# Decode states loaded two steps ahead in a hybrid mLSTM and GLA layer, and side work handed out by a budget that carries its overdraft

## The chip, the cores and the metric

The kernel runs on one core of a Trainium2 chip. The metric is the device time of one execution in microseconds (us); the median of three runs of the kernel before is 846.66 us.

## The reference

One inference step of one layer for 256 prompt tokens and 8 decode tokens (one for each of 8 sequences), all in float32. `p = x @ w_in` feeds two recurrent branches; cut to what matters:

```python
# mLSTM branch: 4 heads, 256x256 matrix memory C for each head
qk = silu(conv(qk_pre)); q, k = split(qk); k = k * 256 ** -0.5
C_new = dec * C + einsum('bhs,bhsd,bhse->bhde', wk, k, v)
num   = decay * einsum('bhtd,bhde->bhte', q, C) + einsum('bhts,bhse->bhte', s, v)
h     = num / maximum(abs(den), exp(-m_t))
# GLA branch: 4 heads, 128x256 state S for each head, decay per key channel
S_new = exp(last) * S + einsum('bhsd,bhse->bhde', k * exp(last - bc), v)
o     = einsum('bhtd,bhde->bhte', q * exp(bc), S) + einsum('bhts,bhse->bhte', a, v)
# each branch: headwise norm, gate, projection; merge, output projection, layer norm
ya = (norm(h) * sigmoid(a_o) * silu(a_z)) @ w_pa
yb = (norm(o) * silu(b_z)) @ w_pb
y  = (sigmoid(g_a) * ya + sigmoid(g_b) * yb) @ w_out
out = layernorm(ALPHA * x + y)
```

For the 8 decode tokens the states C (8 x 4 x 256 x 256, 8 MB) and S (8 x 4 x 128 x 256, 4 MB) are read, updated with one token's key and value, multiplied with its query, and written back.

## The kernel before, in words

**Main work.** All tokens (264 columns: 256 prompt, 8 decode) stand as columns. The projections are 129 units, each one 128-row tile of outputs over 2048 inputs (the one called `small` is narrower): 16 `qk`, 1 `small`, 8 `av`, 4 `bq`, 4 `bk`, 8 `bv`, 16 `ao`/`az` in turns, 8 `bz`, 32 `ga`/`gb` in turns, 16 `pab`, 16 `out`; they are counted from 0 here. A unit's weights come as two pieces of 128x1024 float32. A piece goes through four engines: SP loads it (`load_raw`, line 181, tile `raw`, 4 buffers), ScalarE rounds it to the matmul's format (`hi`, line 203), VectorE takes the difference (`lo`, line 204), and TensorE multiplies hi by x_hi, hi by x_lo and lo by x_hi (lines 223, 224, 227): 48 matmuls a unit. Weights are cast three pieces (`LA`) ahead of the unit that uses them.

**Side work.** After each unit `pump(BUDGET)` runs the generators that are open, one step each, as long as the budget lasts; a step ends at a `yield`, which names its cost. Generators that are not in `BACK` go first, then up to `BACK_STEPS` (2) steps of the first one in `BACK`, which are the two decode generators. What a step overdraws is forgotten at the next unit:

```python
for g in [g for g in side if g.__name__ not in BACK]:
    if budget > 0:
        with tc.high_priority(offset=SIDE_PRIO):
            budget -= step(g)
```

The generators that matter here: `e_v`'s inner `g` transposes a value tile (`vT`, a ScalarE copy at line 394) on TensorE (line 401); `g_a_prompt` is the mLSTM of the prompt; `g_a_decode` the mLSTM decode (16 chunks of C, tile `cch`, scaled on ScalarE at line 546, updated and multiplied with the query on VectorE at lines 562 and 564); `g_gla_prompt` the GLA of the prompt, whose levels halve the tile: at each level TensorE multiplies at line 698 what VectorE scaled at line 705 in the step before; `g_gla_decode` the GLA decode (8 chunks of S, tile `sch`, four VectorE operations of 128x512 for each half chunk, lines 802 to 805); `g_a_norm` and `g_b_norm` the headwise norms (their statistics go through TensorE at lines 627, 639 and 824).

**What sets the order.** TensorE executes in the order of the program text (`MANUAL`): a side matmul stands behind the unit in whose pump it was issued. On the other engines and the DMA queues a scheduler orders instructions by priority before the kernel runs (`PRIO` 600 for casts, `SIDE_PRIO` 300 for side work outside `BACK`); on the chip each engine then goes through its list in order and waits where the next one isn't ready. Loads are issued by SP, stores of states (`sC`, `sS`, `pC`) by POOL.

**Memory.** Large tiles share the pool `b4` with `SLOTS` slots of 4 KB a partition (`t4`); tiles of 2 KB the tag `t2` with 5 buffers. A load into a slot waits until the slot's last user is done. Key and query rows of the decode tokens are written to DRAM and read back into all 128 partitions (`spread_rows`, line 283).

Of the kernel before, what the change touches and what calls it, by code (L numbers as in the profile page):

```python
# [13 lines left out]
F32 = mybir.dt.float32  # L14
# [3 lines left out]
ALU = mybir.AluOpType  # L18
# [16 lines left out]
BUDGET = 2.8  # L35
# [48 lines left out]
def body(ctx, tc, xT, wbig, wsmall, par, cmask, lmask, rowc, gate, wgu, cT, sT, nst, cst, lnr,  # L84
# [51 lines left out]
    wgu_sb = tmp.tile([16, 512], F32, tag="t2", name="wgu_sb", bufs=5)  # L136
    cst_sb = tmp.tile([128, KT, 3, NB], F32, tag="t2", name="cst_sb", bufs=5)
# [148 lines left out]
    def g_gates(ps):  # L286
# [66 lines left out]
        dm = one.tile([16, H, NB], F32, tag="dm", name="dm")  # L353
        V.tensor_tensor(out=dm, in0=r[:, L:T].unsqueeze(1).to_broadcast([16, H, NB]),
                        in1=rc_sb[0:16, 104:104 + H].unsqueeze(2).to_broadcast([16, H, NB]), op=ALU.mult)
        dr = one.tile([16, 2, NB], F32, tag="dr", name="dr")
        V.tensor_copy(out=dr[:, 0], in_=r[:, L:T])
        V.tensor_scalar(out=dr[:, 1], in0=wk[:, L:T], scalar1=K_SCALE, scalar2=None, op0=ALU.mult)
        yield 0.4
# [3 lines left out]
        PE.matmul(pb[:, 0:H * NB], lhsT=ones[0:16, :], rhs=dm.rearrange("p h b -> p (h b)"), start=True, stop=True)  # L363
# [21 lines left out]
    def e_v(ps, j, key, dkey):  # L385
# [23 lines left out]
    def g_a_prompt():  # L409
# [34 lines left out]
        def s3(h):  # L444
# [5 lines left out]
            kw = tmp.tile([128, 2, 256], F32, tag="t2", name="kw", bufs=5)  # L450
# [17 lines left out]
        for h in range(H + 1):  # L468
# [6 lines left out]
            yield 2.0  # L475
# [3 lines left out]
            yield 2.0  # L479
# [3 lines left out]
    def g_a_decode():  # L483
        qT, kT, dw, decb = st["qT"], st["kT"], st["dw"], st["decb"]
        num, dmx, avd = st["num"], st["dmx"], st["avd"]
# [5 lines left out]
        yield 0.5  # L491
        qr = tmp.tile([64, 128], F32, tag="t1", name="qr", bufs=T1_BUFS)
        kr = tmp.tile([64, 128], F32, tag="t1", name="kr", bufs=T1_BUFS)
        nr = tmp.tile([64, 128], F32, tag="t1", name="nr", bufs=T1_BUFS)
        pt = side_ps()
        for x in range(2):
            PE.transpose(out=pt[0:64, x * 128:x * 128 + 128], in_=qkd[:, x].rearrange("p h b t -> p (h b t)"), identity=ident)
        nc.sync.dma_start(out=nr, in_=nst)
        A.copy(out=qr, in_=pt[0:64, 0:128])
        V.tensor_scalar(out=kr, in0=pt[0:64, 128:256], scalar1=dw[:, 1:2], scalar2=None, op0=ALU.mult)  # L500
        kq_d = dram.tile([2, 64, 128], F32, name="kq_d")
        for x, src in enumerate((kr, qr)):
            nc.sync.dma_start(out=kq_d[x], in_=src)
        yield 0.5
# [7 lines left out]
        chunks = {}  # L512

        def load(i):
            if i < 16:
                c = t4([128, 4, 256], "cch")
                nc.sync.dma_start(out=c, in_=cT[i])
                chunks[i] = c

        load(0)  # L520
        yield 0.6
# [6 lines left out]
        yield 0.4  # L528
        scr2 = tmp.tile([128, 256], F32, tag="t1", name="scr", bufs=T1_BUFS)
        steps = [(h, b0, e) for h in range(H) for b0 in (0, 4) for e in range(2)]  # L530
        rows = {}

        def spread(i):

            if i < 16:
                h, b0, _ = steps[i]
                rows[h, b0] = t4([128, 4, 256], "kb"), t4([128, 4, 256], "qb")
                for x in range(2):
                    spread_rows(rows[h, b0][x], kq_d[x, 16 * h + 2 * b0:16 * h + 2 * b0 + 8, :])
# [8 lines left out]
        spread(0)  # L548
        scale(0)
        yield 1.6  # L550
        for i, (h, b0, e) in enumerate(steps):
            if e == 0:
                spread(i + 2)
            if i:
                G.dma_start(out=sC[i - 1], in_=chunks.pop(i - 1))
            if i + 1 < 16:
                scale(i + 1)
            kb, qb = rows[h, b0]
            c = chunks[i]
            nd = num.t(2 * h + e)  # L560
            for b in range(4):
                V.scalar_tensor_tensor(out=c[:, b, :], in0=kb[:, b, :], scalar=avd[:, 2 * h + e, b0 + b:b0 + b + 1],  # L562
                                       in1=c[:, b, :], op0=ALU.mult, op1=ALU.add)
                V.scalar_tensor_tensor(out=scr2, in0=c[:, b, :], scalar=1.0, in1=qb[:, b, :], op0=ALU.mult,  # L564
                                       op1=ALU.mult, accum_out=nd[:, L + b0 + b:L + b0 + b + 1])
                if b % 2:
                    yield 2.1
        G.dma_start(out=sC[15], in_=chunks.pop(15))
# [46 lines left out]
    def g_a_norm():  # L615
# [8 lines left out]
        for h in range(H):  # L624
# [4 lines left out]
            sq = tmp.tile([128, 2, T], F32, tag="t2", name="nsq", bufs=5)  # L629
# [23 lines left out]
    def g_gla_rows():  # L653
        gq, gk, la = st["gq"], st["gk"], st["la"]
        gd = one.tile([128, 3, H, NB], F32, tag="gd", name="gd")
        A.activation(out=gd[:, 0], in_=la[:, :, L:T], func=AF.Exp, scale=TAU_INV)
        V.tensor_copy(out=gd[:, 1], in_=gk[:, :, L:T])
        V.tensor_copy(out=gd[:, 2], in_=gq[:, :, L:T])
        yield 0.4
        pt = side_ps()  # L660
        PE.transpose(out=pt[0:96, 0:128], in_=gd.rearrange("p x h b -> p (x h b)"), identity=ident)
# [7 lines left out]
    def g_gla_prompt():  # L669
# [19 lines left out]
        for l in range(7):  # L689
# [16 lines left out]
            B2 = tmp.tile([128, H, n2], F32, tag="t2", name="gB", bufs=5)  # L706
            V.tensor_tensor(out=B2, in0=Bv[:, :, :, 0], in1=Bv[:, :, :, 1], op=ALU.add)
            E = tmp.tile([128, H, n2], F32, tag="t2", name="gE2", bufs=5)
            A.activation(out=E, in_=B2, func=AF.Exp, scale=TAU_INV)
            B, nb = B2, n2  # L710
            if hs == 32:
                for s0, n0 in ((0, 0), (64, 32)):
                    A.copy(out=am[s0:s0 + 32, :, s0 + 32:s0 + 64], in_=pl[s0:s0 + 32, :, n0:n0 + 32])
                yield 2.0
                continue
            if hs == 64:
                A.copy(out=am[0:64, :, 64:128], in_=pl[0:64])
                yield 2.0
# [8 lines left out]
            yield 3.0  # L727
# [3 lines left out]
        a01 = tmp.tile([128, 4, 128], F32, tag="t2", name="a01", bufs=5)  # L731
# [12 lines left out]
        for hh in range(2):  # L744
# [6 lines left out]
            pc = tmp.tile([128, 512], F32, tag="t2", name="pc", bufs=5)  # L751
# [14 lines left out]
    def g_gla_decode():  # L766
# [9 lines left out]
        load(0)  # L776
        yield 0.1
        spread = {}

        def rows_of(h):  # L780
            if h < H:
                spread[h] = [t4([128, NB, 128], "g" + x) for x in "akq"]
                for i, x in enumerate(spread[h]):
                    spread_rows(x, rows[32 * i + 8 * h:32 * i + 8 * h + 8, :])

        rows_of(0)
        yield 0.1
        for h in range(H):
            rows_of(h + 1)
            ab, kb, qb = spread.pop(h)  # L790
            for bh in range(2):
                load(2 * h + bh + 1)
                c = chunks.pop(2 * h + bh)
                b0 = 4 * bh
                for p in (0, 2):
                    q, cc, sh = slice(b0 + p, b0 + p + 2), c[:, p:p + 2], [128, 2, 2, 128]
                    kv, pr = (tmp.tile(sh, F32, tag="t2", name=x, bufs=5) for x in ("gkv", "gpr"))
                    for i in range(2):
# [500 lines left out]
```

## Time and profile before

| what | value |
|---|---|
| runs, us | 845.08, 846.66, 847.56 (median 846.66) |
| profiled execution, us | 846.17 |
| its span, first to last instruction, us | 844.3 |
| TensorE busy in the span | 819.3 us (97%) |
| VectorE busy | 592.8 us (70%) |
| ScalarE busy | 450.1 us (53%) |
| DMA traffic | 186.30 MB, mean 221 GB/s |

The profile takes one execution apart; what follows is read against its 844.3 us of span, and 1.87 us lie around the span. "Wait" means time in which an engine stood still in front of an instruction, and the row names what ended it. The clock column is the TensorE clock that was granted, 1.00 being 2.4 GHz.

### The profile page before, as it was taken

Reading aid. Unit: us, or ns where it says so; the run is one execution under the profiler, and the core shown is the slowest. Engines: PE = TensorE matmul, PEld = TensorE weight load, DVE = VectorE, ACT = ScalarE, POOL = GpSimd, SP = SyncE. Lnnn points to the kernel's source line nnn. Section 1 sums busy time; section 2 is a strip of 40 time slices with the busy share of each in tenths; the row PEclk is TensorE's granted clock in tenths of the full one; section 3 lists DMA queues with packets and bytes.
Section 4 is the critical chain, followed back from the end, with each engine's and each line's share of the span. In section 5 each row is a group of like instructions: output and inputs, shape, how many; then the busy total and the mean of one; then the engine's idle time right before and its main releaser. Section 6 shows DMA issues by size and latency. Waiting matters only on the chain.

```text
span 844.3 us, 16681 instructions
## 1 busy us (share of the span) xinstructions
PE 819.3 (97%) x6749; PEld 809.2 (96%) x6749; DVE 592.8 (70%) x967; ACT 450.1 (53%) x700; POOL 45.8 (5%) x75
## 2 busy tenths in 40 slices
PE   6999999999999899999999999899999999999996
PEld 6999999999999899999999999799999999999995
DVE  6977668655748888767489979984445676666962
ACT  5755457545544653555376758564444444444633
POOL 0000000000100000000000000400000000000410
PEclk9999999999999999999999999999999999999998
DMA  9765555867679985678776987665555555576513
GB/s 318 252 193 183 159 187 172 233 201 266 227 262 291 339 305 184 227 244 305 250 273 180 354 319 258 200 203 186 177 182 189 179 177 179 188 250 205 180 47 103
DMA packets 55237, 186.30 MB, mean 221 GB/s; under 512 B 8292, under 2 KB 9256, under 8 KB 55160
## 3 DMA queue, kind: packets, MB, share of 16 engines
q1 hardware_dynamic: 51032, 170.82, 62.3%
q0 software_dynamic: 4128, 14.42, 4.3%
q8 instruction: 53, 0.87, 0.4%
q14 instruction: 24, 0.20, 0.1%
HBM read 168.50 MB, written 16.71 MB: 219 GB/s over the span
## 4 chain that ended last, share of the span: by engine, by line
PE 79%; DMA 8%; DVE 7%; issue 3%; ACT 1%; SPq 0%; POOL 0%; ACTq 0%; POOLq 0%; DVEq 0%
PE mm L223 25%; PE mm L224 24%; PE mm L227 24%; DMA cch<-cT 4%; DVE lo L204 3%; DMA raw<-wbig 2%; DMA sch<-sT 2%; DMA pC<-pc 1%; DVE scr L564 1%; DVE gpr L804 1%; PE sd L698 1%; ACT hi L203 1%; DVE cch L562 1%; DVE sch L803 1%; ACT cch L546 0%
## 5 line engine op out<-in xcount | busy, mean ns | idle before, releaser
L223 PE MATMUL mm<-xh,hi 128*128 128x264 f32 x1552 | 446.8, 288 | 7.3 <-ACT hi L203 7.3
L224 PE MATMUL mm<-xl,hi 128*128 128x264 f32 x1552 | 440.9, 285 | 0.0
L227 PE MATMUL mm<-xh,lo 128*128 128x264 f32 x1536 | 436.9, 284 | 0.0
L203 ACT CAST hi<-raw 128x1024 fp32r<-128x1024 f32 (+1 forms) x260 | 267.8, 1034 | 288.3 <-PE mm L224 243.3
L204 DVE TENSOR_TENSOR lo<-raw,hi 128x1024 fp32r<-128x1024 f32 (+1 forms) x260 | 315.1, 1214 | 139.2 <-ACT hi L203 137.2
L223 PEld LDWEIGHTS mm<-xh,hi 128*128 128x128 f32 x1552 | 293.8, 189 | 8.9 <-ACT hi L203 7.3
L224 PEld LDWEIGHTS mm<-xl,hi 128*128 128x128 f32 x1552 | 293.9, 189 | 0.3
L227 PEld LDWEIGHTS mm<-xh,lo 128*128 128x128 f32 x1536 | 289.7, 189 | 0.2 <-DVE lo L204 0.2
L223 PE MATMUL mm<-mh,hi 128*128 128x264 f32 x256 | 72.9, 285 | 0.0
L227 PE MATMUL mm<-mh,lo 128*128 128x264 f32 x256 | 72.6, 284 | 0.0
L224 PE MATMUL mm<-ml,hi 128*128 128x264 f32 x256 | 72.4, 283 | 0.0
L224 PEld LDWEIGHTS mm<-ml,hi 128*128 128x128 f32 x256 | 48.1, 188 | 0.0
L223 PEld LDWEIGHTS mm<-mh,hi 128*128 128x128 f32 x256 | 48.1, 188 | 0.0
L227 PEld LDWEIGHTS mm<-mh,lo 128*128 128x128 f32 x256 | 48.1, 188 | 0.0
L546 ACT ACTIVATE cch<-cch,decb 128x256 f32<-128x256 f32 x64 | 27.8, 500 | 35.1 <-DMA cch<-cT 35.1
L562 DVE SCALAR_TENSOR_TENSOR cch<-kb,avd,cch 128x256 f32<-128x256 f32 x64 | 29.5, 480 | 20.4 <-ACT cch L546 17.8
L227 PE MATMUL mm<-ybh,lo 128*128 128x264 f32 x128 | 36.4, 284 | 0.0
L227 PE MATMUL mm<-yah,lo 128*128 128x264 f32 x128 | 36.3, 284 | 0.0
L224 PE MATMUL mm<-ybl,hi 128*128 128x264 f32 x128 | 36.3, 284 | 0.0
L223 PE MATMUL mm<-ybh,hi 128*128 128x264 f32 x128 | 36.3, 284 | 0.0
L223 PE MATMUL mm<-yah,hi 128*128 128x264 f32 x128 | 36.3, 284 | 0.0
L224 PE MATMUL mm<-yal,hi 128*128 128x264 f32 x128 | 36.2, 283 | 0.0
(310 smaller groups left out, 807.2 us busy)
## 6 DMA issues: line engine op xcount, KB each, us to landing
raw<-wbig SPq DMA_DIRECT2D x252, 512.0 KB, 4.7
cch<-cT SPq DMA_DIRECT2D x16, 512.0 KB, 8.8
sC<-cch POOLq DMA_DIRECT2D x16, 512.0 KB, 5.7
kb<-kq_d SPq DMA_DIRECT2D x8, 512.0 KB, 7.4
qb<-kq_d SPq DMA_DIRECT2D x8, 512.0 KB, 8.0
sch<-sT SPq DMA_DIRECT2D x8, 512.0 KB, 7.4
sS<-sch POOLq DMA_DIRECT2D x8, 512.0 KB, 6.0
xr<-xT SPq DMA_DIRECT2D x4, 528.0 KB, 6.9
```

Source lines behind the costliest of these rows:

```text
L203: A.copy(out=h, in_=r)
L204: V.tensor_tensor(out=lo, in0=r, in1=f(h), op=ALU.subtract)
L223: PE.matmul(out, lhsT=wh, rhs=rh, start=(k == k0), stop=False)
L224: PE.matmul(out, lhsT=wh, rhs=rl, start=False, stop=small and k == k1 - 1)
L227: PE.matmul(out, lhsT=los[n, k], rhs=rh, start=False, stop=(k == k1 - 1))
L546: A.activation(out=c[:, b, :], in_=c[:, b, :], func=AF.Copy, scale=decb[:, h, b0 + b:b0 + b + 1])
L562: V.scalar_tensor_tensor(out=c[:, b, :], in0=kb[:, b, :], scalar=avd[:, 2 * h + e, b0 + b:b0 + b + 1], in1=c[:, b, :], op0=ALU.mult, op1=A ...
L564: V.scalar_tensor_tensor(out=scr2, in0=c[:, b, :], scalar=1.0, in1=qb[:, b, :], op0=ALU.mult, op1=ALU.mult, accum_out=nd[:, L + b0 + b:L + ...
L698: PE.matmul(pl[s0:s0 + m, 4 * hf + h, n0:n0 + w].rearrange("p (n s) -> p n s", s=hs), lhsT=K[:, h, hf * 128 + s0:hf * 128 + s0 + m], rhs=r ...
L803: V.tensor_tensor(out=cc, in0=cc, in1=kv, op=ALU.add)
L804: V.tensor_tensor(out=pr, in0=cc, in1=qb[:, q].unsqueeze(2).to_broadcast(sh), op=ALU.mult)
```

## The change

It sets `SLOTS` 20 to 19, `T2_BUFS` 5 to 7, `BUDGET` 2.8 to 3.4. `pump` carries a negative rest over to the next unit (`credit`), and a step of a `BACK` generator with a negative cost ends the pump at once. In the mLSTM decode a chunk now holds 2 sequences with both halves of a head's values (before: 4 sequences with one half); its key and query rows come in one tile `kq` for each chunk (before: `kb` and `qb` for every second chunk). The chunk's load is issued two steps ahead of its use instead of one, that of its rows one chunk ahead; the scale of a chunk is 2 ScalarE instructions of 128x512 instead of 4 of 128x256. The key is no longer scaled by `K_SCALE * wk`; that factor goes into `avd`. In the GLA decode a chunk's rows come as `gak` (decay and key, 512 KB) and `gqr` (query, 256 KB, from `t2`) instead of `ga`, `gk`, `gq` (512 KB each) for two chunks, and chunks are loaded two steps ahead instead of one. `e_v`'s `g` yields twice with cost 0 before the transposes instead of once, `g_a_prompt` yields 1.5 instead of 2.0, the levels of `g_gla_prompt` 2.5 and 1.7 instead of 3.0 and 2.0, `g_g` 0.3 instead of 1.9.

```diff
-BUDGET = 2.8
+BUDGET = 3.4
-SLOTS = 20
+SLOTS = 19
+T2_BUFS = 7
...
     def e_v(ps, j, key, dkey):
...
         def g():
+            yield 0.0
             yield 0.0
             pt = side3(2, 128)
...
     def g_a_decode():
...
+        kqo = tmp.tile([128, 16, 2, 4], F32, tag="t1", name="kqo", bufs=T1_BUFS)
+        for x in range(2):
+            V.tensor_copy(out=kqo[:, :, x, :], in_=qkd[:, 1 - x].rearrange("p h (c b) t -> p (h c) (b t)", b=2))
+        V.tensor_tensor(out=avd.rearrange("p (h e) b -> p h e b", e=2), in0=avd.rearrange("p (h e) b -> p h e b", e=2),
+                        in1=wkb.unsqueeze(2).to_broadcast([128, H, 2, NB]), op=ALU.mult)
+        yield -0.5
...
+        PE.transpose(out=pt[:, 256:384], in_=kqo.rearrange("p a x c -> p (a x c)"), identity=ident)
...
+        load(0)
+        load(1)
+        yield -0.6
...
+        spread(0)
+        yield -1.0
         pb = side_ps()[:, 0:H * NB]
         PE.matmul(pb, lhsT=ones[0:64, :], rhs=dx, start=True, stop=True)
...
-            load(i + 1)
-            c = chunks[i]
-            for b in range(4):
-                A.activation(out=c[:, b, :], in_=c[:, b, :], func=AF.Copy, scale=decb[:, h, b0 + b:b0 + b + 1])
...
+                for b in range(2):
+                    A.activation(out=chunks[i][:, b], in_=chunks[i][:, b], func=AF.Copy, scale=decb[:, h, b0 + b:b0 + b + 1])
...
+        for i in range(16):
+            h, b0 = i // 4, i % 4 * 2
             if i:
-                G.dma_start(out=sC[i - 1], in_=chunks.pop(i - 1))
...
+                G.dma_start(out=sC[i - 1], in_=chunks.pop(i - 1).rearrange("p b e k -> p (b e) k"))
+            load(i + 2)
+            spread(i + 1)
+            scale(i + 1)
...
+                yield 2.1
...
     def g_gla_decode():
...
+                spread[i] = t4([128, 2, 4, 128], "gak"), tmp.tile([128, 4, 128], F32, tag="t2", name="gqr", bufs=T2_BUFS)
...
+        for i in range(8):
+            h, b0 = i // 2, i % 2 * 4
+            rows_of(i + 1)
+            load(i + 2)
...
+    credit = [0.0]
+
     def pump(budget):
+        credit[0] = budget = min(credit[0], 0.0) + budget
...
                 if budget > 0:
-                    budget -= step(g)
+                    c = step(g)
+                    budget -= abs(c)
+                    if c < 0:
+                        credit[0] = budget
+                        return
+        credit[0] = budget
```

How the change moves instructions shows at three places. The first is TensorE after unit 28 (`bq3`), where the small matmul that sums the decode normaliser (`dx`) stands at the end of the prompt's side work. Before:

```order
L435 MATMUL sd<-E,avt 128x256
L436 MATMUL sd<-E,avt 128x128
L437 MATMUL sd<-E,ones 128x256
L438 MATMUL sd<-E,ones 128x128
L461 MATMUL sd<-avt,kw 128x257 x4
L523 MATMUL sd<-dx,ones 128x32
```

Now, at the same place and, behind 48 + 7 + 48 further matmuls and the next head's first steps, after unit 30:

```order
L439 MATMUL sd<-E,avt 128x128
L440 MATMUL sd<-E,ones 128x256
L441 MATMUL sd<-E,ones 128x128
L464 MATMUL sd<-avt,kw 128x257 x4
L505 MATMUL sd<-par_sb,kqo 128x128
L507 MATMUL sd<-par_sb,qkd 64x128 x2
...
L441 MATMUL sd<-E,ones 128x128
L464 MATMUL sd<-avt,kw 128x257 x4
L540 MATMUL sd<-dx,ones 128x32
```

The matmul of `dx` has moved two units back, and the transposes of the query and key rows stand where it was.

The second is ScalarE over the `bv` units, where the copies `vT` stand between casts (`hi`) and the scales of the mLSTM chunks (`cch`). Before:

```order
L203 CAST hi<-raw 128x1024
L546 ACTIVATE cch<-cch,decb 128x256 x4
L203 CAST hi<-raw 128x1024
L394 COPY vT<-mm 128x256
L546 ACTIVATE cch<-cch,decb 128x256
L203 CAST hi<-raw 128x1024
L546 ACTIVATE cch<-cch,decb 128x256 x3
L203 CAST hi<-raw 128x1024
L394 COPY vT<-mm 128x256
L546 ACTIVATE cch<-cch,decb 128x256 x4
```

Now:

```order
L204 CAST hi<-raw 128x1024 x2
L396 COPY vT<-mm 128x256
L204 CAST hi<-raw 128x1024
L551 ACTIVATE cch<-cch,decb 128x512 x2
L204 CAST hi<-raw 128x1024
L396 COPY vT<-mm 128x256
L551 ACTIVATE cch<-cch,decb 128x512 x2
```

Between the casts each copy had up to eight scales, of two chunks, ahead of it; now one chunk's two scales stand between two copies, but they still stand ahead of the copy.

The third is SP's queue over the same units, with the loads of weights (`raw`), of chunks (`cch`) and of row tiles. Before:

```order
L181 DMA raw<-wbig 128x1024 x5
L517 DMA cch<-cT 128x1024
L283 DMA kb<-kq_d 128x1024
L283 DMA qb<-kq_d 128x1024
L517 DMA cch<-cT 128x1024
L181 DMA raw<-wbig 128x1024 x2
L517 DMA cch<-cT 128x1024
```

Now:

```order
L182 DMA raw<-wbig 128x1024 x6
L519 DMA cch<-cT 128x1024
L284 DMA kq<-kq_d 128x1024
L519 DMA cch<-cT 128x1024
L284 DMA kq<-kq_d 128x1024
L182 DMA raw<-wbig 128x1024 x4
L519 DMA cch<-cT 128x1024
L284 DMA kq<-kq_d 128x1024
```

Four loads of decode data still stand together between loads of weights; each is still 512 KB.

## Rows read from the trace of the kernel before

**Rows 1.** The page: busy time of the engines, share of the span, instructions.
```profile
PE 819.3 (97%) x6749; PEld 809.2 (96%) x6749; DVE 592.8 (70%) x967; ACT 450.1 (53%) x700; POOL 45.8 (5%) x75
```
**Rows 2.** All waits of TensorE: engine, line, what ended the wait, us in total, times, longest.
```profile
PE mm L223 <- ACT hi L203: 7.3, 1, 7.3
PE sd L824 <- DVE ns L819: 3.6, 2, 2.5
PE sd L401 <- ACT vT L394: 3.4, 2, 2.5
PE sd L698 <- DVE gq L705: 2.6, 1, 2.6
PE sd L523 <- ACT pnn L464: 0.8, 1, 0.8
```
**Rows 3.** Stretches of 20 us: busy us and instructions of PE, PEld, DVE, ACT, POOL, then granted clock, DMA share, GB/s.
```profile
260.00:280.00 20.00, 17.41 (x143) 16.99 (x141) 13.36 (x34) 9.20 (x16) 1.07 (x2) 1.00 0.92 325
280.00:300.00 20.00, 19.16 (x147) 19.16 (x148) 19.53 (x49) 11.96 (x20) 1.59 (x3) 0.91 0.95 334
440.00:460.00 20.00, 20.00 (x168) 20.00 (x167) 20.00 (x23) 12.49 (x18) 0.53 (x1) 1.00 0.65 207
460.00:480.00 20.00, 20.00 (x168) 20.00 (x167) 20.00 (x28) 13.45 (x25) 0.53 (x1) 1.00 0.87 303
520.00:540.00 20.00, 16.45 (x127) 15.66 (x126) 19.76 (x23) 14.66 (x26) 8.35 (x8) 1.00 0.74 233
560.00:580.00 20.00, 20.00 (x168) 20.00 (x167) 10.53 (x10) 10.36 (x14) 0.00 (x0) 1.00 0.64 206
```
**Rows 4.** TensorE in order of time from 277.9 to 285.7: start, us, line, what; in brackets the idle time before it and what ended it.
```profile
278.04 0.28 PE L227 MATMUL mm<-xh,lo 128*128 128x264 f32 x1
280.84 0.44 PE L401 MATMUL sd<-par_sb,vT 128*128 128x128 f32 x2 [2.52 <-ACT vT L394]
281.24 0.28 PE L224 MATMUL mm<-xl,hi 128*128 128x264 f32 x1
281.36 0.29 PE L227 MATMUL mm<-xh,lo 128*128 128x264 f32 x1
...
282.22 0.42 PE L223 MATMUL mm<-xh,hi 128*128 128x264 f32 x1
282.44 0.42 PE L224 MATMUL mm<-xl,hi 128*128 128x264 f32 x1
...
285.30 0.42 PE L227 MATMUL mm<-xh,lo 128*128 128x264 f32 x1
285.52 0.32 PE L223 MATMUL mm<-xh,hi 128*128 128x264 f32 x1
```
**Rows 5.** ScalarE in order of time from 269 to 282, the stretch ahead of that stall.
```profile
270.76 1.05 ACT L203 CAST hi<-raw 128x1024 fp32r<-128x1024 f32 x1 [2.61 <-DMA raw<-wbig]
277.88 1.71 ACT L546 ACTIVATE cch<-cch,decb 128x256 f32<-128x256 f32 x4 [6.06 <-DMA cch<-cT]
279.49 1.03 ACT L203 CAST hi<-raw 128x1024 fp32r<-128x1024 f32 x1
280.42 0.36 ACT L394 COPY vT<-mm 128x256 f32<-128x256 f32 x1
```
**Rows 6.** Waits of ScalarE and of VectorE, as in rows 2.
```profile
ACT cch L546 <- DMA cch<-cT: 35.1, 12, 7.3
DVE cch L562 <- ACT cch L546: 17.8, 6, 5.3
DVE gB L707 <- DMA pC<-pc: 8.2, 1, 8.2
DVE sch L802 <- DMA sch<-sT: 4.9, 3, 3.9
```
**Rows 7.** DMA issues: engine, count, KB each, median us from issue to landing.
```profile
raw<-wbig SPq DMA_DIRECT2D x252, 512.0 KB, 4.7
cch<-cT SPq DMA_DIRECT2D x16, 512.0 KB, 8.8
kb<-kq_d SPq DMA_DIRECT2D x8, 512.0 KB, 7.4
```
**Rows 8.** VectorE in order of time ahead of the GLA level's stall.
```profile
315.10 0.69 DVE L705 TENSOR_TENSOR gk<-gk,gE 128x512 f32<-128x512 f32 x1
315.70 1.22 DVE L204 TENSOR_TENSOR lo<-raw,hi 128x1024 fp32r<-128x1024 f32 x1
316.83 0.69 DVE L705 TENSOR_TENSOR gq<-gq,gE 128x512 f32<-128x512 f32 x1
```
**Rows 9.** VectorE in order of time ahead of the second norm's stalls.
```profile
529.75 0.69 DVE L805 TENSOR_REDUCE oT<-gpr 128x4 f32<-128x512 f32 x1
530.36 2.12 DVE L204 TENSOR_TENSOR lo<-raw,hi 128x1024 fp32r<-128x1024 f32 x1
532.40 1.11 DVE L819 TENSOR_TENSOR ns<-nsq 128x264 f32<-128x264 f32 x3
534.56 0.97 DVE L819 TENSOR_TENSOR ns<-nsq 128x264 f32<-128x264 f32 x1
```
**Rows 10.** Groups of instructions by line: what, form, count, busy us, mean ns of one.
```profile
L546 ACT ACTIVATE cch<-cch,decb 128x256 f32<-128x256 f32 x64 | 27.8, 500 | 35.1 <-DMA cch<-cT 35.1
L762 ACT COPY oT<-sd 128x512 f32<-128x512 f32 x4 | 2.3, 584 | 0.3
L804 DVE TENSOR_TENSOR gpr<-sch,gq 128x512 f32<-128x512 f32 x16 | 11.0, 687 | 0.2
L401 PE MATMUL sd<-par_sb,vT 128*128 128x128 f32 x32 | 6.2, 276 | 3.4 <-ACT vT L394 3.4
```
**Rows 11.** Waits of SP's queue, as in rows 2 (the queue stands in front of a load).
```profile
SPq L181 <- DVE lo L204: 457.8, 180, 11.0
SPq L283 <- DMA sS<-sch: 7.6, 2, 5.7
```

More of the change, by code (lines that the diff above doesn't have):

```diff
@@ L358, in g_gates @@
         V.tensor_scalar(out=dr[:, 1], in0=wk[:, L:T], scalar1=K_SCALE, scalar2=None, op0=ALU.mult)
+        dm = one.tile([16, 2, H, NB], F32, tag="dm", name="dm")
+        for w in range(2):
+            V.tensor_tensor(out=dm[:, w], in0=dr[:, w].unsqueeze(1).to_broadcast([16, H, NB]),
+                            in1=rc_sb[0:16, 104:104 + H].unsqueeze(2).to_broadcast([16, H, NB]), op=ALU.mult)
         yield 0.4
@@ L498, in g_a_decode, with load, spread @@
         nc.sync.dma_start(out=nr, in_=nst)
+        A.copy(out=kq, in_=pt[:, 256:384])
         A.copy(out=qr, in_=pt[0:64, 0:128])
         V.tensor_scalar(out=kr, in0=pt[0:64, 128:256], scalar1=dw[:, 1:2], scalar2=None, op0=ALU.mult)
[L501 to L504, printed above, removed]
+        kq_d = dram.tile([128, 128], F32, name="kq_d")
+        nc.sync.dma_start(out=kq_d, in_=kq)
+        chunks, rows = {}, {}
+        def load(i):
+            if i < 16:
+                chunks[i] = t4([128, 2, 2, 256], "cch")
+                nc.sync.dma_start(out=chunks[i].rearrange("p b e k -> p (b e) k"), in_=cT[i])
+        def spread(i):
+            if i < 16:
+                rows[i] = t4([128, 2, 2, 256], "kq")
+                spread_rows(rows[i].rearrange("p x b k -> p (x b) k"), kq_d[8 * i:8 * i + 8, :])
+        load(0)
+        load(1)
+        yield -0.6
         dn = one.tile([64, 1], F32, tag="dn", name="dn")
@@ L527, in g_a_decode, with scale @@
         V.tensor_tensor(out=dmx[:, :, L:T], in0=dmx[:, :, L:T], in1=ad, op=ALU.max)
-        yield 0.4
         scr2 = tmp.tile([128, 256], F32, tag="t1", name="scr", bufs=T1_BUFS)
-        steps = [(h, b0, e) for h in range(H) for b0 in (0, 4) for e in range(2)]
-        rows = {}
-        def spread(i):
+        def scale(i):
             if i < 16:
[L536 to L539, printed above, removed]
@@ L551, in g_a_decode @@
-        for i, (h, b0, e) in enumerate(steps):
-            if e == 0:
-                spread(i + 2)
+        yield 1.0
+        for i in range(16):
+            h, b0 = i // 4, i % 4 * 2
             if i:
-                G.dma_start(out=sC[i - 1], in_=chunks.pop(i - 1))
[L556 to L567, printed above, removed]
@@ L774, in load, with rows_of @@
                 chunks[i] = c
-        load(0)
[L777 to L784, printed above, removed]
+        spread = {}
+        def rows_of(i):
+            if i < 8:
+                spread[i] = t4([128, 2, 4, 128], "gak"), tmp.tile([128, 4, 128], F32, tag="t2", name="gqr", bufs=T2_BUFS)
+                spread_rows(spread[i][0].rearrange("p x b d -> p (x b) d"), rows[12 * i:12 * i + 8, :])
+                spread_rows(spread[i][1], rows[12 * i + 8:12 * i + 12, :])
@@ new lines, in g_gla_decode @@
+        load(1)
+        yield 0.1
+        for i in range(8):
+            h, b0 = i // 2, i % 2 * 4
+            rows_of(i + 1)
+            load(i + 2)
+            ak, qb = spread.pop(i)
+            c = chunks.pop(i)
+            for p in (0, 2):
+                q, cc, sh = slice(p, p + 2), c[:, p:p + 2], [128, 2, 2, 128]
+                kv, pr = (tmp.tile(sh, F32, tag="t2", name=x, bufs=T2_BUFS) for x in ("gkv", "gpr"))
+                for b in range(2):
+                    for e in range(2):
+                        A.activation(out=kv[:, b, e, :], in_=ak[:, 1, p + b, :], func=AF.Copy,
+                                     scale=bvd[:, 2 * h + e, b0 + p + b:b0 + p + b + 1])
+                V.tensor_tensor(out=cc, in0=cc, in1=ak[:, 0, q].unsqueeze(2).to_broadcast(sh), op=ALU.mult)
+                V.tensor_tensor(out=cc, in0=cc, in1=kv, op=ALU.add)
+                V.tensor_tensor(out=pr, in0=cc, in1=qb[:, q].unsqueeze(2).to_broadcast(sh), op=ALU.mult)
+                V.tensor_reduce(out=oT.h(h)[:, :, L + b0 + p:L + b0 + p + 2].rearrange("p e b -> p b e"), in_=pr,
+                                axis=mybir.AxisListType.X, op=ALU.add)
+                yield 2.6
+            G.dma_start(out=sS[i], in_=c)
@@ L842, in g_g @@
         gtiles[q] = raw
-        yield 1.9
+        yield 0.3
     def e_pab(pa, pb, j):
```

105 lines of the change are left out of this document (39 added, 66 removed).

## The prediction

> **What bounds the kernel now.** First the busy times: TensorE has work in 819.3 of 844.3 us, VectorE in 592.8, ScalarE in 450.1 [rows 1]. So the kernel is TensorE's stream of weight matmuls, and a change to side work can gain only what TensorE loses between its matmuls. The waits of TensorE say what that is [rows 2]: 7.3 us at the start, until the first weights have arrived and been cast, and four lines in the middle, 3.6 + 3.4 + 2.6 + 0.8 = 10.4 us in six stalls. No weight matmul waits after the start: all six are side matmuls that stand in TensorE's fixed order ahead of something late. The stretches say where: TensorE's busy time falls below 20 in 260:280, 280:300 and 520:540 among those shown, and the clock column falls once, to 0.91 in 280:300 [rows 3].
>
> That clock has a price of its own. After the 2.52 us stall before 280.84 matmuls start every 0.12 us (281.24, 281.36); from 282.22 they start every 0.22 us, until 285.52 [rows 4]. These 3.30 us hold 15 starts, which take 15 x 0.12 = 1.8 us at the full rate: 1.5 us lost. It is the lower level, 1.2 GHz. The 2.5 us stall of 520:540 leaves the column at 1.00 [rows 3], so a stall of this size may or may not cost it.
>
> The causes, one by one. *The transposes of vT (3.4 us).* ScalarE finishes a cast, then stands 6.06 us in front of the scale of a chunk until `cch` arrives at 277.88; behind it in its list wait a cast and the copy `vT`, at 280.42; the transposes start at 280.84 [rows 5, 4]. ScalarE spends 35.1 us in such waits, the longest 7.3; they hand VectorE 17.8 us of waiting [rows 6], because a chunk takes 8.8 us from issue to landing, against 4.7 for a weight piece [rows 7]. *The GLA level (2.6 us).* TensorE wants `gq`, which VectorE starts at 316.83, behind `gk` and a `lo` [rows 8]; VectorE is behind because it had waited for `cch` and once 8.2 us for the store of `pC` to free a buffer [rows 6]. *The second norm (3.6 us).* `ns` starts at 532.40 and 534.56, each behind a `lo` and the last GLA decode operations [rows 9]; VectorE has been full, 20.00 of 20 in 440:480 and 19.76 in 520:540 [rows 3]. *The sum of dx (0.8 us).* The matmul is issued in the same step as the VectorE operations that make its input; the row's releaser is an unrelated copy [rows 2].
>
> **The change, part by part.**
>
> *dx:* its matmul now stands two units behind its old place, and the VectorE operations one: a unit of 48 matmuls at 0.12 us [rows 4], 5.8 us, lies between them where there was nothing. A wait of 0.8 us becomes 5 us to spare. Minus 0.8.
>
> *The transposes:* the second empty step moves every pair one unit back while the copy stays, so the copy may come 5.8 us later than before. The worst was 2.5 us late; 3.3 us are to spare. The stall returns only if ScalarE waits 6.06 + 3.3 = 9.4 us at one place; its longest wait in the whole kernel is 7.3 [rows 6]. I do not count on the chunks arriving earlier. In the text a load is two steps ahead; in the order the scale still stands soon behind its load, with two chunks and two row tiles issued together, as four tiles were before. The bytes are the same 16 + 16 loads of 512 KB. Minus 3.4, and minus 1.5 for the clock, which fell behind this stall alone.
>
> *The Trainium skill on this:* the page "DMA: Bandwidth & Descriptors", section "Anatomy of one DMA — SWDGE (gpsimd) path", fits one transfer of POOL's queue as 2.0 us plus bytes over 436 GB/s, which makes an estimated 3.2 us of 512 KB. By it the loads would hardly ever be late, all that hangs on them would vanish, and the time would be about 0.7 us under mine. The 8.8 us here is for SP's queue with other transfers around, and it decides.
>
> *The GLA levels:* the generator starts one unit later, as `bvt` is done one unit later; VectorE's work for it can start when it did. 2.6 us late against 5.8 us of delay leaves 3.2 us to spare, less if VectorE waits longer for `cch` than it did. The bounds are 0 and the old 2.6; 3.2 us is nearer to 0, I take 0.2. The `pC` wait of 8.2 us I leave in: two more `t2` buffers may shorten it, and nothing in the sum needs that.
>
> *The second norm:* a half chunk of the GLA decode is four VectorE operations of 0.687 us [rows 10], 2.75 us, and a unit's two `lo` are 2 x 1.22 = 2.4 us [rows 8]. Before, a step of cost 2.6 leaves 0.2 of 2.8, so a second one runs and the overdraft is forgotten: two half chunks a unit, 7.9 us of VectorE against 5.8 us of TensorE, 2.1 us lost a unit. Now the overdraft carries: 3.4 / 2.6 = 1.3 half chunks a unit, 2.4 + 3.6 = 6.0 us, 0.2 us lost a unit. VectorE comes to the norm nearly level. The decode and the norm end some eight units later, in a stretch where VectorE has 10.53 us of 20 to do [rows 3], and before the first `pab` unit. Bounds 0 and 3.6; I take 0.3.
>
> *The first norm, new:* GLA decode steps now run beside it, and the mLSTM decode that must end before it is thinner and five units longer. VectorE then has a half chunk, two `lo` and the norm's own operations in one unit, somewhat over 5.8 us, for about three units. `ns` for the last head may be late for its matmul. Nothing like it stands in the trace; the nearest rows are the second norm's, 3.6 us in two stalls, as the upper bound, and 0 as the lower. It is three units, not the whole decode: I take 0.5.
>
> *Small things.* TensorE gets one more transpose of 128x128 (276 ns busy for the like [rows 10]) and two more places where a side matmul breaks the weight stream; the break at 280.84 took 0.40 us to the next start after it with two transposes in it [rows 4], so together 0.3 us. Scales of 128x512 instead of 128x256: a copy of 128x512 takes 584 ns against 500 for a scale of 128x256 [rows 10], so 32 x 0.58 = 19 us replace 27.8, and ScalarE, with half its time free, gains 9 us that nobody waits for. Extra copies of the rows and the factor in `avd` cost VectorE about 1 us in all, in units with room. `g_a_prompt`'s and `g_g`'s cheaper steps only open the budget.
>
> *Slots.* SP now holds three chunks and two row tiles, five slots, against two chunks and up to four row tiles, six; one slot fewer in the pool balances that. In the GLA decode it is three chunks and two `gak` against two chunks and six row tiles. I count nothing.
>
> **The sum.** 844.3 - 10.4 - 1.5 + 0.2 + 0.3 + 0.5 + 0.3 = 833.7 us of span, and 1.9 us around it: 835.6. The profiled execution (846.17) stands 0.5 us under the median of the runs, so the comparison with the median is a little kinder than the sum.
>
> **The rivals.**
>
> *One or two stalls stay.* ScalarE still has the scale ahead of the copy, and chunks still come four loads at a time. For it: the waits of 35.1 us, and a first norm that has more to do. Against: every stalled matmul has a unit more, and no wait seen eats it. One stall of 2.5 us with the clock behind it is 4.0 us: 839.6; two are 843.6.
>
> *The change does not do what it says.* The scheduler, not the text, places loads; if chunks arrive later against their scales than now, ScalarE's waits grow past 9.4 us, the vT and level stalls come back at their old size with the clock, and the norms meet a late VectorE: 844 to 849. For it: the loads are as many and stand as close. Against: the second norm's stall and that of dx hang on no load, and they are 4.4 us.
>
> *Slower: SP's queue stands.* All loads go through one queue in order. If a row tile or chunk two steps ahead finds no free slot (its last user is stored by POOL), the weight loads behind it wait too. SP has stood 5.7 us in front of a row tile until `sS` was stored, and up to 11.0 us in its ordinary waits, without a weight matmul waiting [rows 11, 2]. Three cast pieces (8.6 us of TensorE, half a unit each) and those in `raw` behind them cover at least that. The price is each microsecond beyond it, and 1.5 us of clock for each such stall. It decides from 849.2, 13.6 us over my sum: with 8.6 us of cover, one block of some 21 us (8.6 + 13.6 - 1.5), or three of 12. Five slots against six speaks against it, nineteen against twenty for it.
>
> **Chances.** 0.3% of 846.66 is 2.5 us, about what a measurement of this kernel can tell from no change: the band is 844.1 to 849.2. My forecast, 833.5 to 838: 0.59. One or two stalls stay, 838 to 844.1: 0.23. It does not do what it says, in the band: 0.11. Slower by the queue: 0.07. Faster 0.82, same 0.11, slower 0.07. The range begins at 833.5, 0.8 under a kernel without any middle stall (834.3, less the spread of runs), and goes to 845.5 to take in most of the two middle cases; the likeliest one's own is 833.5 to 838.
>
> **What would show it.** In the waits of TensorE the lines of vT, `gq`, dx and the second `ns` should be gone or under 0.5 us each, with a first-norm line of at most 1 us. The clock column should be 1.00 until the last stretch. ScalarE's wait for `cch` should still be there, 20 to 40 us, which would show that cover was added and not that loads came earlier. VectorE should be under 20 of 20 in the stretches between 460 and 560. SP should show no wait much over 11 us in the decode. The prediction is wrong if a weight matmul waits after the start, if the first norm stalls by 3 us or more, or if stalls of vT and `gq` stay although their matmuls stand a unit later.

## The result and the profile after

The kernel after takes 835.2 us (median of 4 runs, 833.88 to 835.83), the kernel before 847.11 us (845.08 to 847.74) beside it: a ratio of 0.9861, 95% interval 0.9840 to 0.9882. The forecast was 835.6 us. The span of the profiled execution is 833.2 us, 11.1 us under that of before. A second set of runs of the same kernel gave 834.27 us (ratio 0.9854, 0.9828 to 0.9881).

The time came from where the waits of TensorE had been. All its waits after the change (engine, line, what ended the wait, us in total, times, longest):

```profile
PE mm L224 <- ACT hi L204: 7.4, 1, 7.4
PE sd L702 <- DVE gq L709: 1.0, 1, 1.0
PE sd L642 <- DVE ns L635: 0.5, 1, 0.5
```

Of the four lines in the middle of [rows 2], those of vT, dx and the second norm are gone; `gq` is down from 2.6 to 1.0, and the first norm has a line of 0.5. The balance: 10.4 - 1.5 = 8.9 us of waits less. The stretches of 20 us, to be held against [rows 3] (busy us and instructions of PE, PEld, DVE, ACT, POOL, then granted clock, DMA share, GB/s):

```profile
260.00:280.00 20.00, 20.00 (x168) 20.00 (x167) 11.94 (x26) 9.85 (x14) 0.54 (x1) 1.00 0.87 301
280.00:300.00 20.00, 20.00 (x169) 20.00 (x169) 16.71 (x45) 10.12 (x14) 1.39 (x3) 1.00 0.88 313
300.00:320.00 20.00, 19.01 (x202) 18.61 (x202) 19.83 (x35) 11.05 (x15) 0.74 (x2) 1.00 0.70 238
440.00:460.00 20.00, 19.50 (x149) 18.66 (x148) 17.00 (x27) 13.36 (x26) 0.50 (x1) 1.00 0.81 290
460.00:480.00 20.00, 20.00 (x168) 20.00 (x167) 20.00 (x23) 14.40 (x24) 0.03 (x1) 1.00 0.60 198
520.00:540.00 20.00, 20.00 (x168) 20.00 (x167) 15.16 (x20) 10.59 (x22) 1.07 (x2) 1.00 0.92 303
560.00:580.00 20.00, 20.00 (x161) 19.74 (x160) 16.45 (x15) 14.62 (x21) 5.70 (x5) 1.00 0.75 238
```

The clock column is 1.00 in 280:300, where it was 0.91; that is the 1.5 us which the prediction put on it. Of the 11.1 us by which the span fell, 0.7 are in neither item and stay unexplained. VectorE's work of 520:540 has moved on: 15.16 there instead of 19.76, and 16.45 instead of 10.53 in 560:580.

Waits of ScalarE and VectorE (against [rows 6]):

```profile
ACT cch L551 <- DMA cch<-cT: 39.4, 14, 6.1
DVE cch L566 <- DMA kq<-kq_d: 37.0, 13, 6.2
DVE gB L711 <- DMA pC<-pc: 2.5, 1, 2.5
```

The loads, with count, KB each and median us to landing (against [rows 7]):

```profile
raw<-wbig SPq DMA_DIRECT2D x252, 512.0 KB, 4.8
cch<-cT SPq DMA_DIRECT2D x16, 512.0 KB, 6.9
kq<-kq_d SPq DMA_DIRECT2D x16, 512.0 KB, 8.2
```

ScalarE waits for chunks as much as before (39.4 against 35.1), and VectorE now waits 37.0 us for row tiles where it had waited 17.8 behind ScalarE. So both engines wait more for decode data than before, and TensorE waits less.

### The profile page after: what moved, and what is told of

Same layout as the page of the kernel before. It is cut to its first block, busy times and chain, and to the rows that moved or that the text cites. A ratio compares the mean times of both kernels' runs of the same rounds, so it can differ in the third digit from the quotient of the medians.

```text
span 833.2 us, 16677 instructions
## 1 busy us (share of the span) xinstructions
PE 817.1 (98%) x6750; PEld 807.6 (97%) x6750; DVE 593.2 (71%) x971; ACT 444.8 (53%) x669; POOL 44.4 (5%) x75
## 4 chain that ended last, share of the span: by engine, by line
PE 94%; DVE 2%; DMA 2%; issue 1%; ACT 0%; ACTq 0%; SPq 0%; POOLq 0%; POOL 0%; DVEq 0%
PE mm L224 29%; PE mm L225 29%; PE mm L228 29%; DMA gak<-rows_d 1%; DVE lo L205 1%; PE sd L464 1%; PE sd L702 1%; DMA raw<-wbig 1%; PE sd L423 1%; PE sd L404 0%; PE sd L438 0%; PE sd L753 0%; PE sd L996 0%; PE sd L312 0%; PE sd L964 0%
## 5 line engine op out<-in xcount | busy, mean ns | idle before, releaser
L566 DVE SCALAR_TENSOR_TENSOR cch<-kq,avd,cch 128x256 f32<-128x256 f32 x64 | 29.1, 480 | 37.0 <-DMA kq<-kq_d 37.0
L551 ACT ACTIVATE cch<-cch,decb 128x512 f32<-128x512 f32 x32 | 21.6, 718 | 39.4 <-DMA cch<-cT 39.4
```

The source lines that it names most:

```text
L551: A.activation(out=chunks[i][:, b], in_=chunks[i][:, b], func=AF.Copy, scale=decb[:, h, b0 + b:b0 + b + 1])
L566: V.scalar_tensor_tensor(out=c[:, b, e], in0=r[:, 0, b], scalar=avd[:, j, b0 + b:b0 + b + 1], in1=c[:, b, e], op0=ALU.mult, op1=ALU.add)
```

## The experiments

Theory 1 (cover) is the prediction's: stalls go because the waiting matmuls stand a unit later, and the carried overdraft spreads the GLA decode. Theory 2 (supply): decode data come earlier. Theory 3 (rate) was formed after the first four runs.

**One step ahead instead of two.**

```diff
-        load(1)
...
-            load(i + 2)
+            load(i + 1)
```

> The kernel after, with chunks of both decodes loaded one step ahead instead of two; the order of TensorE's matmuls is that of the kernel after. Theory 1 (cover: the stalls went because the waiting matmuls stand a unit later and the GLA decode is spread out): 835.2 us within 1.5; TensorE's waits in the middle stay under 2.5 us in sum (1.5 in the kernel after), although ScalarE's wait for cch grows beyond 39 us. Theory 2 (supply: the stalls went because decode data arrive earlier): 838 to 843, with a line for vT or gq of 2 us or more.

835.61 us (834.76 to 836.66), ratio 0.9869 (0.9832 to 0.9906). Its time can't be told from that of the kernel after (835.2). TensorE's wait besides the start, and VectorE's and ScalarE's for loads:

```profile
PE mm L228 <- DVE lo L205: 1.4, 2, 0.9
...
DVE cch L565 <- DMA kq<-kq_d: 16.3, 8, 4.3
DVE sch L805 <- DMA sch<-sT: 13.4, 5, 6.1
...
ACT cch L550 <- DMA cch<-cT: 27.4, 15, 4.7
```

Theory 2 falls for vT and `gq`: neither line came back. Theory 1 is left standing here; the next run takes its cover away. What was expected of ScalarE was wrong: it waited less with loads one step ahead, 27.4 us. New is a wait of weight matmuls for `lo`, in the GLA decode, where VectorE waited 13.4 us for `sch`.

**One empty step instead of two.**

```diff
         def g():
-            yield 0.0
             yield 0.0
```

> The kernel after, with one empty step ahead of the transposes of vT instead of two, so that these and the GLA levels stand one unit earlier again. Theory 1 (cover): a line of 1 to 4 us for vT comes back in TensorE's waits, the gq line grows from 1.0 to 3 or more, and where a stall of 2.5 us halves the clock 1.5 us more: 838 to 842. Theory 2 (supply): neither line comes, 835.2 within 1.5.

833.89 us (833.52 to 834.19), ratio 0.9848 (0.9812 to 0.9884); no wait of TensorE is listed but the start. Theory 1 falls for vT and `gq`: in the kernel after there is no stall without the unit of cover either.

**No overdraft carried over, budget 2.8.**

```diff
-BUDGET = 3.4
+BUDGET = 2.8
...
-        credit[0] = budget = min(credit[0], 0.0) + budget
```

> The kernel after, with the budget of before: 2.8, and no overdraft carried over. Theory 1 (the overdraft spreads the GLA decode, and VectorE comes level to the second norm): VectorE is at 20.00 of 20 up to the second norm, its line in TensorE's waits is 2 to 4 us, 837 to 840. Theory 2 (the smaller and earlier loads of the GLA decode freed VectorE): no such line, 835.2 within 1.5.

845.57 us (844.04 to 848.55), ratio 0.9981 (0.9960 to 1.0002): nearly the whole gain is gone. TensorE's waits besides the start (one of 0.2 us for `lo` is left out):

```profile
PE sd L702 <- DVE gq L709: 4.2, 1, 4.2
PE sd L829 <- DVE ns L824: 2.0, 1, 2.0
PE sd L702 <- DVE gq L688: 0.8, 1, 0.8
```

The second norm came as expected, 2.0 us. The 5.0 us of `gq` were not expected, since the level matmuls still stood a unit later, and the time lies well above the 837 to 840 expected. Two stretches show the lower clock behind these stalls, 0.66 and 0.57:

```profile
320.00:330.00 10.00, 9.43 (x78) 9.39 (x79) 7.50 (x11) 4.89 (x6) 0.00 (x0) 0.66 1.00 363
...
528.00:532.00 4.00, 4.00 (x19) 3.87 (x20) 4.00 (x3) 3.97 (x7) 1.68 (x2) 0.57 0.70 215
```

**The kernel before with the order alone** (second empty step, budget 3.4, carry).

```diff
-BUDGET = 2.8
+BUDGET = 3.4
...
+            yield 0.0
             yield 0.0
...
+        credit[0] = budget = min(credit[0], 0.0) + budget
...
+        credit[0] = budget
```

> The kernel before, with two empty steps ahead of the transposes of vT, the budget of 3.4 and the overdraft carried over; chunks, row tiles, loads one step ahead, 20 slots and the place of the dx matmul are those of before. Theory 1 (cover and spread): vT 3.4, gq 2.6, second norm 3.6 and clock 1.5 go, dx 0.8 stays: 836 to 838. Theory 2 (supply): less than half of the gain, 842 or more.

839.6 us (834.82 to 842.6), ratio 0.9902 (0.9872 to 0.9933), between the two expectations.

```profile
PE mm L227 <- DVE lo L204: 3.6, 3, 3.0
PE sd L699 <- DVE gq L706: 0.9, 1, 0.9
PE sd L524 <- ACT pnn L465: 0.8, 1, 0.8
```

vT and the second norm are gone and dx stays, as theory 1 has it, but this run changes cover and rate together. A line is new: weight matmuls wait 3.6 us for `lo`.

**Theory 3.** What the carry changes first is not the GLA decode but the mLSTM decode: before, a cost of 2.1 against 2.8 lets two steps run in every unit that has little else, and the overdraft is forgotten. Then ScalarE has scales and VectorE updates of two steps in its list where one unit's time is available, and both are late for vT and for the levels. The next three runs set it against theory 1.

**The second empty step alone, in the kernel before.**

```diff
+            yield 0.0
             yield 0.0
```

> The kernel before, with one thing changed: a second empty step ahead of the transposes of vT, which moves these and the GLA levels one unit back on TensorE. Theory 1 (cover): the vT line, the gq line and the clock stretch go, 7.5 us, the second norm (3.6) and dx (0.8) stay: 839 to 841. Theory 3 (rate: the mLSTM decode at two steps a unit puts ScalarE and VectorE behind, and the overdraft that is carried over cuts that): vT gets its cover, but VectorE is as far behind as before and the gq line stays at 2 us or more, with or without a clock stretch: 842 to 845.

845.25 us (842.61 to 849.6), ratio 0.9974 (0.9957 to 0.9991).

```profile
PE sd L825 <- DVE ns L820: 4.6, 1, 4.6
PE sd L699 <- DVE gq L706: 4.0, 1, 4.0
PE sd L699 <- DVE gq L685: 1.0, 1, 1.0
PE sd L524 <- ACT pnn L465: 0.8, 1, 0.8
```

The vT line is gone, 3.4 us, and the time is handed on: `gq` has 5.0 instead of 2.6, the second norm 4.6 instead of 3.6. TensorE, no longer held up by vT, starts the levels at 294.4 us, as before (294.5), although they stand a unit later, and VectorE is no further. The execution that was profiled is the slowest of the ten, 849.6 us, so these waits are larger than in most; the median says the same, 2.1 us less instead of the 6 to 8 of theory 1. Theory 3.

**The carry and the budget alone, in the kernel before.**

```diff
-BUDGET = 2.8
+BUDGET = 3.4
...
+        credit[0] = budget = min(credit[0], 0.0) + budget
...
+        credit[0] = budget
```

> The kernel before, with the budget of 3.4 and the overdraft carried over, and nothing else; TensorE has the transposes of vT and the GLA levels where they were. Theory 1 (cover): the second norm's 3.6 us go, vT 3.4, gq 2.6, the clock's 1.5 and dx 0.8 stay: 842 to 845. Theory 3 (rate): vT and gq are under 1 us each as well, and what is left is dx, and weight matmuls that wait for lo in the GLA decode as in the run with both parts (3.6 us and the clock): 837 to 841.

840.19 us (838.87 to 842.64), ratio 0.9918 (0.9889 to 0.9948). TensorE's waits besides the start, and VectorE's in the GLA decode:

```profile
PE mm L227 <- DVE lo L204: 3.5, 2, 3.0
PE sd L523 <- ACT pnn L464: 0.8, 1, 0.8
...
DVE sch L802 <- DMA sch<-sT: 20.9, 4, 8.6
```

vT, `gq` and the second norm are all gone, and the trace has the transposes of vT and the level matmuls behind as many weight matmuls as in the kernel before, so these two were given no cover. (The second norm does stand later, since the decode before it takes longer.) The budget of 3.4 alone was not run in the kernel before. Theory 3.

**The rest of the change alone** (layout, row tiles, loads two steps ahead, slots, dx).

```diff
-BUDGET = 3.4
+BUDGET = 2.8
...
         def g():
-            yield 0.0
             yield 0.0
...
-        credit[0] = budget = min(credit[0], 0.0) + budget
```

> The kernel after, with one empty step ahead of the transposes, the budget of 2.8 and no overdraft carried over: chunks of two sequences, row tiles for each chunk, loads two steps ahead, 19 slots and the later dx matmul are what is left of the change. Theory 1 (cover) and theory 3 (rate) both: lines for vT or gq of 4 us or more in sum, and one for the second norm of 2 us: 844 to 850. Theory 2 (supply): under 840.

846.13 us (842.4 to 848.69), ratio 0.9983 (0.9959 to 1.0007): no gain that can be told. TensorE's waits besides the start (one of 0.2 us for `bvt` is left out):

```profile
PE sd L828 <- DVE ns L823: 4.3, 3, 2.9
PE sd L701 <- DVE gq L708: 4.3, 2, 3.5
PE sd L403 <- ACT vT L396: 1.4, 1, 1.4
```

This run also settles a rival for `gq`, VectorE's wait for the store of `pC` (8.2 us in [rows 6]): here no such wait is listed, and `gq` still has 4.3 us; before with the carry alone it is 5.8 us, and there is no `gq` line.

**The kernel after, again.**

> The kernel after, unchanged, beside the others on one chip: 835.2 us within 1, gq line between 0 and 2 us.

834.27 us (833.73 to 835.67); no wait of TensorE after the start is listed, so its 1.0 for `gq` and 0.5 for the first norm come and go between executions.

**One decode step a unit, in the kernel before.**

```diff
-BUDGET = 2.8
+BUDGET = 3.4
-BACK_STEPS = 2
+BACK_STEPS = 1
```

> The kernel before, with a budget of 3.4 and at most one step of a decode generator a unit (BACK_STEPS 1); nothing is carried over. As a side effect the dx matmul stands where the kernel after has it. Theory 3 (rate: it is two decode steps in one unit that put ScalarE and VectorE behind): the lines of vT, gq and the second norm are under 1 us each, and no weight matmul waits for lo, since one half chunk and two lo are 5.2 us of VectorE against 5.8 us a unit: 834 to 837. Theory 1 (cover) would leave vT, gq and the clock: 841 or more.

841.21 us (839.74 to 841.64), ratio 0.9928 (0.9902 to 0.9954).

```profile
PE mm L227 <- DVE lo L204: 2.9, 3, 1.5
PE mm L224 <- DVE ybl L210: 1.0, 1, 1.0
PE mm L223 <- ACT ybh L209: 0.8, 1, 0.8
PE mm L223 <- ACT gr L582: 0.6, 1, 0.6
```

The stalls of vT, `gq` and the second norm are gone, as theory 3 said; that no weight matmul would wait was wrong, and so were the 834 to 837 us expected. The time is where theory 1 had it, 841 or more, but with none of the lines that it named. Weight matmuls wait for `lo` in the GLA decode, where VectorE waited 17.6 us for `sch`, and the first `pab` unit waits for `ybh` and `ybl`. That a decode slowed this far ends too close to its reader is read from the order and was not tested.

**Carry, and GLA chunks two steps ahead, in the kernel before.**

```diff
...
         rows_of(0)
+        load(1)
         yield 0.1
...
-                load(2 * h + bh + 1)
+                load(2 * h + bh + 2)
```

> The kernel before with the budget of 3.4 and the overdraft carried over, as in the run before_credit (840.2 us), and with the GLA decode's chunks loaded two steps ahead. If the 3.5 us in which weight matmuls waited for lo there, and the clock stretch behind them, came from chunks loaded one step ahead (VectorE waited 20.9 us for sch, once 8.6): they go, dx stays, 835 to 837. If they came from the row tiles or from VectorE's load alone: 839 to 842.

836.6 us (835.08 to 838.86), ratio 0.9883 (0.9851 to 0.9915), against 840.19 with the carry alone.

```profile
PE mm L227 <- DVE lo L204: 2.0, 2, 1.6
PE sd L523 <- ACT pnn L464: 0.8, 1, 0.8
...
DVE sch L803 <- DMA sch<-sT: 17.3, 4, 7.1
```

The clock stretch behind the 3.0 us stall (0.91 in 580:600 with the carry alone, 1.00 now) is gone, and 1.5 of the 3.5 us of waits. The two were not timed side by side. One wait of 7.1 us stays, so the load's place in the text explains a part; what holds the rest (the three row tiles, the slots) was not taken apart.

**The larger budget without the carry, in the kernel after.**

```diff
-        credit[0] = budget = min(credit[0], 0.0) + budget
```

> The kernel after with its budget of 3.4, but with no overdraft carried over. Theory 3 (rate) in the form that the carry and not the larger budget does it: two steps a unit come back, gq and the second norm have lines of 2 us or more each, 843 to 849. If the larger budget does it: 834 to 837.

851.82 us (851.28 to 854.05), ratio 1.0065 (1.0041 to 1.0090): slower than before, with the whole rest of the change in place, and above the 843 to 849 expected. TensorE's waits besides the start:

```profile
PE sd L702 <- DVE gq L709: 7.4, 3, 5.8
PE sd L829 <- DVE ns L824: 5.7, 2, 5.0
```

**One decode step a unit instead of the carry, in the kernel after.**

```diff
-BACK_STEPS = 2
+BACK_STEPS = 1
...
-        credit[0] = budget = min(credit[0], 0.0) + budget
```

> The kernel after with the budget of 3.4, no carry, and at most one step of a decode generator a unit. Theory 3 (rate): a fixed cap does what the carried overdraft does, no line over 1 us in TensorE's waits after the start, 833 to 836, not to be told from the kernel after. Otherwise 840 or more, as without the carry.

832.51 us (832.08 to 833.87), ratio 0.9836 (0.9803 to 0.9870); just under the 833 to 836 expected; no wait of TensorE is listed but the start, 7.0 us. A fixed cap does what the carry does. Its median is 1.8 to 2.7 us under the two medians of the kernel after; the ranges of single runs touch (833.87 and 833.73), and the two were not timed side by side, so it is not slower and has the lowest median of all runs here; that it is faster than the kernel after is not shown.

**What VectorE had been given.** The number that separates these runs is how many of the mLSTM decode's updates (64 in all) VectorE executes in 240:316, the stretch ahead of the GLA levels. The rows are VectorE's busy time with that line alone, in the kernel before, the kernel after, before with the carry alone, and after with the larger budget and no carry:

```profile
240.00:316.00 76.00, 14.70 (x32) 0.98 0.86 302
```
```profile
240.00:316.00 76.00, 10.96 (x24) 1.00 0.81 281
```
```profile
240.00:316.00 76.00, 9.22 (x20) 1.00 0.80 267
```
```profile
240.00:316.00 76.00, 14.44 (x32) 1.00 0.85 305
```

| kernel | updates in 240:316 | gq, us | second norm, us | median, us |
|---|---|---|---|---|
| before | 32 | 2.6 | 3.6 | 847.11 |
| before, two empty steps | 28 | 5.0 | 4.6 | 845.25 |
| after, rest alone | 32 | 4.3 | 4.3 | 846.13 |
| after, no carry, 2.8 | 28 | 5.0 | 2.0 | 845.57 |
| after, no carry, 3.4 | 32 | 7.4 | 5.7 | 851.82 |
| before, carry alone | 20 | 0 | 0 | 840.19 |
| before, order alone | 20 | 0.9 | 0 | 839.6 |
| after | 24 | 1.0 | 0 | 835.2 |
| after, one step a unit | 20 | 0 | 0 | 832.51 |

With 20 to 24 the levels wait 1.0 us at most, with 28 or 32 2.6 or more. The runs left out of the table agree: after again 24, after with one step ahead 24, after with one empty step 20, before with one step a unit 20, before with carry and GLA chunks two steps ahead 20, all without a `gq` line. Within a group the number does not order the times. The carry was switched in both kernels (in the kernel before together with the budget of 3.4), and a cap on the steps does the same in both, so that a slower decode removes these stalls is shown; whether through VectorE's own time or through the loads that more updates call for was not separated.

## Why the prediction was right, and where it was not

**The frame was right.** Only TensorE's waits and the clock behind them were to be had, 11.9 us; the span fell by 11.1, and the left-over waits, 1.5 us, are close to the 1.0 that the sum kept; the first norm's 0.5 came as forecast, and in the second profile neither it nor `gq` is there. Put together from runs that were not timed side by side, the carry with its budget gives about 7.2 us of the gain (847.37 to 840.19), GLA chunks two steps ahead 3.6 more (836.6), and some 1.4 stay with the rest of the change, 0.8 of them the size of the dx line.

**The second norm: right in direction, its rates were not.** The carry thins the GLA decode, the norm's line is gone, and without the carry it is back. Its matmuls stand eight units later, as forecast: they start at 569.5 us instead of 533.0, and VectorE has their last `ns` done at 560.3. But the prediction took VectorE at 20.00 of 20 as a decode that saturates it, and the rows don't bear that out for the whole stretch. In the kernel before VectorE begins 14 half chunks in 460:520 and in the kernel after 12 in 480:560 (VectorE's busy time with the first operation of a half chunk alone), which is 1.4 and 0.9 a unit of 5.8 us, not two and 1.3. VectorE isn't full in 480:500 before, and in the full stretch 460:480 after no half chunk begins:

```profile
460.00:520.00 60.00, 9.60 (x14) 1.00 0.88 309
480.00:560.00 80.00, 8.08 (x12) 1.00 0.88 303
480.00:500.00 20.00, 20.00 (x168) 20.00 (x167) 15.45 (x22) 12.32 (x29) 1.06 (x2) 1.00 0.90 325
460.00:480.00 20.00, 0.00 (x0) 1.00 0.60 198
```

What fills 460:480 after, and 440:460 before, is `lo` and the first norm (four reciprocals, 7.0 and 7.2 us). So the sign that VectorE should be under 20 of 20 between 460 and 560 failed for a reason that has nothing to do with the decode.

**The transposes and the levels: right terms, wrong cause.** The sum took 3.4, 2.4 and 1.5 us for the unit of cover, 7.3 of the 11.1. That they came out is luck: the cover by itself does not earn them, and with the carry it is not needed. In the kernel after that cover is worth nothing that can be measured (833.89 without it); in the kernel before it moves the vT stall on to `gq` and the norm, and the time falls by 2 us, not by the 7.3 that these terms promise. The step that failed is "what is late next": it was asked for each stall by itself, with the other engines' progress held fixed, while a stall removed upstream takes the time away that VectorE used to catch up. The carry was counted for the GLA decode and not for the mLSTM decode, where the same arithmetic holds (2.1 against 2.8: two steps in a unit that has little else, overdraft forgotten). Nor did the sign that was to show cover, ScalarE's wait for `cch` still being there, show it: the wait is there, and without the cover the stalls are gone as well.

**dx was right:** its line is gone wherever the matmul moved, and stands at 0.8 us in every run where it did not.

**The loads: half right.** That chunks would still be waited for was right (39.4 us, within the 20 to 40 named); with the lead of one step ScalarE waits 27.4. By the fit in the Trainium skill's page "DMA: Bandwidth & Descriptors", section "Anatomy of one DMA — SWDGE (gpsimd) path", which is for POOL's queue, these loads would land in an estimated 3.2 us. On SP's queue 6.9 and 8.2 were measured, so the trace decided against it once more. Not seen was that the carry alone would leave 3.5 us and a clock stretch in the GLA decode, where loads two steps ahead are worth up to 3.6 us (840.19 to 836.6). In the kernel after, whose row tiles are smaller, the lead of two steps in both decodes is worth 0.4 us (835.61 to 835.2), less than can be told. So the lead paid in the kernel before with the carry; in the mLSTM decode no run shows that it does.

**A term off in size, at no cost.** The scales of 128x512 were put at 0.58 us by the nearest copy. They take 0.718, 21.6 us in all instead of 19 (the group's row: count, busy us, mean ns, idle time before):

```profile
L551 ACT ACTIVATE cch<-cch,decb 128x512 f32<-128x512 f32 x32 | 21.6, 718 | 39.4 <-DMA cch<-cT 39.4
```

ScalarE has the time, and nothing followed from it. The `pC` wait, left in at 8.2 us, is down to 2.5, and nothing in the sum hung on it.

**The rivals.** A stall or two staying did not happen in the kernel after beyond the 1.0 us of `gq`, where at most 0.5 was expected; the order alone ended there (839.6). The rest alone (846.13) ended where the prediction had the change that does not do what it says. SP's queue did not decide: its longest wait in the decode was 8.9 us, for `scr`. The side that would have made it slower was another one, which the prediction did not name: the larger budget without the carry costs 17 us against the kernel after.

## What to carry to other kernels

Where side work is handed out by a budget, look at what happens to the overdraft: a rule that forgets it lets the costliest steps run faster than was meant (here up to 32 updates in 76 us where the carry leaves 20 to 24), and what waits behind them is late. A stall removed by cover alone went to the next matmuls that need a late engine, so sum the late engine's work over the stretch before counting each stall's gain. Loads issued earlier in the text paid here only in one kernel's GLA decode, where weight matmuls waited behind them.

## What the runs showed of the hardware

The size of a stall did not tell whether the lower clock follows. In the kernel after without carry the stall of 2.0 us before the second norm was followed by a clock of 0.57 in 528:532 (above). In the run with the rest alone the `gq` stall of 3.5 us was followed by full clock; its stretch and the next one:

```profile
310.00:316.00 6.00, 2.53 (x45) 2.31 (x43) 5.96 (x13) 3.38 (x4) 0.53 (x1) 1.00 0.88 290
316.00:322.00 6.00, 6.00 (x56) 5.86 (x55) 5.92 (x9) 2.34 (x2) 0.00 (x0) 1.00 0.61 167
```

In the kernel before with one decode step a unit, two stalls of 0.8 and 1.0 us in front of a `pab` unit, at 637.9 and 639.3, were followed by 0.61:

```profile
640.00:644.00 4.00, 4.00 (x24) 4.00 (x23) 2.12 (x4) 1.46 (x2) 0.00 (x0) 0.61 0.39 125
```

A price of 1.5 us for each stall, as two of the rivals used it, is therefore neither an upper nor a lower bound: the stall of 3.5 us cost none, and the 0.66 over the 10 us of 320:330 above is an estimated (1 - 0.66) x 10 = 3.4 us lost.
